# Hybrid DeltaNet and attention block: SBUF start addresses of the matmul operands, byte 0 or byte 32 of a 64-byte line

## The chip, the cores and the metric

The kernel runs on one core of one Trainium2 chip. The metric is device time in microseconds of one execution. Before the change three runs took 1934.67, 1937.08 and 1939.23 us, the median is 1937.08.

## What is computed

One layer of a backbone over 1024 latent tokens with a prefix of 256 context tokens, model width 1024, all in float32. A modulated RMS norm feeds one wide input projection; its columns go to two branches, whose outputs are gated, merged and projected once more.

```python
h  = rms_norm(x)   * (1 + scale)   + shift        # 1024 latent tokens
hc = rms_norm(ctx) * (1 + scale_c) + shift_c      # 256 context tokens
qkv_a, z_a, a_raw, b_raw, q_b, k_b, v_b, z_b, gates = split_cols(h @ w_in)
o_a = gdn_bidirectional(...)     # short conv on q, k, v, then a chunked gated delta rule, both ways, 8 heads
o_b = diff_attend(q, k, v, lam)  # softmax(q1 k1) - lam * softmax(q2 k2), times v, 8 heads, 1280 keys
merged = g_a * (y_a @ w_oa) + g_b * (y_b @ w_ob)
x + gate * (merged @ w_out)
```

## The kernel before

A float32 product is made from three matmuls of float32r operands (the type that TensorE streams faster than float32): each operand is split into a high part and a low part, and high·high, high·low and low·high are summed in one PSUM bank. ScalarE makes the high part with a copy, VectorE or GpSimd the low part with a subtraction. So most matrix tiles come in pairs: `wh` and `wl` (weights), `hs` (two tiles, the normed tokens turned to columns), `ah` and `al` (the softmax weights turned), `vh` and `vl` (values).

Every matmul has two operands in SBUF. The stationary one, 128 columns, is loaded into the array by an instruction of its own (LDWEIGHTS; the profile has it on PEld): this is the *loaded* operand. The other one is *moving*: it is streamed through in 256 or 512 columns (288 for one tile of weights that carries 32 gate columns). Tiles hold float32, so 16 columns are 64 bytes of a partition.

The stages overlap, in this order:

- **Front** (`front`, line 238): loads, RMS norm (`x`), turns through TensorE (`pt`, line 63), modulation with fp32 matmuls of the tile `wa` against `pad` (`mp`), first projection.
- **Convolution** (`conv_flow`, line 496): q, k and v columns of the DeltaNet branch. Here the weights are loaded and `hs` moves, in 512 columns (256 for the context). Two pairs of tiles of `self.wab` take the weights in turn (`conv_weights`, line 488). Between them, for the value columns of the attention (kind `"t"`), `hs` is loaded and the weights move, in 256 columns.
- **q, k, v of the attention** (`part_flow`, line 930, weights by `part_weights`, line 898): `hs` is loaded, weights move, 256 columns.
- **Gates and DeltaNet scan** (`fill_flow`, line 906, and `scan`, line 1292): the gate columns' matmuls, `hs` moving in 512 columns, fill the time between small fp32 matmuls of the scan (`chain`, `out`, `gram`, 128 columns), which TensorE runs in two passes.
- **Attention** (`scores`, line 1536, and on): `s` (loaded `qh` or `ql`, moving `kk`, 512 or 256 columns), turns of the softmax weights (`t`, loaded `S`), `v` (loaded `vh` or `vl`, moving `ah` or `al`, 256 columns). The `ma` matmuls (moving `y`, 512 columns) are put between them.
- **Last products** (`b_main`, line 1909, and `o_main`, line 2097): `mb`, `x` and `z`, all of 512 columns.

The order of the instructions on each engine is worked out while the program is built, by `flow` and `turn_flow` (lines 75 and 100), from costs written into each step; tiles are handed out by pools, some on the left and some on the right side of SBUF (`side="right"`). A pool's tiles lie behind one another, so the length of an early tile sets the start of all that follow on its side. Two such tiles matter here. `mhalf` (line 203) is the one-column constant of the power function, early on the left side. `kq` (in `keys`, line 1093) is an early tile on the right side, and is allocated 8 columns longer than it is used:

```python
self.mhalf = cp.tile([P, 1], F32, name="mhalf")
...
kq, qk = S("kq", [P, LT + L + 8])[:, :LT + L], S("qk", [P, 2, 2, 2, P])
```

Of the kernel before, what the change touches and what calls it, by code (L numbers as in the profile page):

```python
# [8 lines left out]
F32 = mybir.dt.float32  # L9
F32R = mybir.dt.float32r  # L10
# [7 lines left out]
P = 128  # L18
D = 1024
KT = D // P  # L20
L = 1024
LC = 256
LT = L + LC
# [6 lines left out]
W = 256  # L30
# [13 lines left out]
class Block:  # L44
# [150 lines left out]
    def setup(self):  # L195
        nc, a = self.nc, self.a
        cp = self.cp = self.pool("const")
        self.dp = self.pool("spill", space=DRAM)
        ct = cp.tile([P, 3, P], F32, name="ct")
        nc.sync.dma_start(ct, a["consts"].rearrange("(a p) n -> p a n", p=P))  # L200
        self.ident, self.up, self.lo = (ct[:, i, :] for i in range(3))
        self.one = self.lo[:, 0:1]
        self.mhalf = cp.tile([P, 1], F32, name="mhalf")
        nc.gpsimd.memset(self.mhalf, -0.5)
        self.da = self.dp.tile([H, 2 * NT, 4, 32, 32], F32, name="da")
        self.db = self.dp.tile([H, 2 * NT, 4, 32, 32], F32, name="db")
        self.ya = self.dp.tile([2, H, P, L], F32, name="ya")
        self.yb = self.dp.tile([H, P, L], F32, name="yb")
        self.gkq = self.dp.tile([H, P, LT + L], F32, name="gkq")
        self.gkk = self.dp.tile([H, LT, P], F32, name="gkk")  # L210
        self.gv = self.dp.tile([H, LT, P], F32, name="gv")
        self.sza = self.dp.tile([H, P, L], F32, name="sza")
        self.szb = self.dp.tile([H, P, L], F32, name="szb")
        self.qd = self.dp.tile([2, H, P, L], F32, name="qd")
        self.kd = self.dp.tile([2, H, P, LT], F32, name="kd")
        self.vd = self.dp.tile([2, LT, H * P], F32, name="vd")
        self.gt = self.dp.tile([2 * KT, P, L], F32, name="gt")
        self.ma = self.dp.tile([KT, P, L], F32, name="ma")
        self.xq = self.dp.tile([H, P, 2, NT // 2, 2, 2, P], F32, name="xq")
        self.tbd = self.dp.tile([2, P, 1024], F32, name="tbd")  # L220
        self.gcd = self.dp.tile([2, H, LT], F32, name="gcd")
        self.gad = self.dp.tile([1, D], F32, name="gad")
        self.rbd = self.dp.tile([H, L], F32, name="rbd")
        for n in ("gkq", "gkk", "gv", "sza", "szb", "qd", "kd", "vd", "gt", "gcd", "ya", "yb"):
            self.dbg[n] = getattr(self, n).name


    @staticmethod
    def later(t, us):

        return t[0], t[1] + us

    def bank(self, name):

# [3 lines left out]
    def front(self, st, early, kv0):  # L238

        nc, a, cp, V = self.nc, self.a, self.cp, self.nc.vector  # L240
# [67 lines left out]
        def weights():  # L308
            for i, n in ((0, W), (1, W + 32)):
                yield lambda: (f"w{i}", 1) in T  # L310
                hl, ends = [self.wab[1 - i].tile([P, KT, n], F32R, tag=t, name=t) for t in ("wh", "wl")], []
                for s in range(2):
                    k = slice(s * KT // 2, (s + 1) * KT // 2)
                    for o, rw, us in ((0, raws[s], 0.256), (W, grw[:, k], 0.032))[:1 + i]:
                        c = slice(o, o + rw.shape[2])
                        t1 = yield ACT, 0.1 + 3.6 * us, [T[f"w{i}", s], T.get(("mm", 3))], lambda: nc.scalar.copy(hl[0][:, k, c], rw)
                        t2 = yield DV2, 4.7 * us, [t1], lambda: V.tensor_tensor(
                            hl[1][:, k, c], rw, hl[0][:, k, c].bitcast(F32), ALU.subtract)
                        ends += [t1, t2]
                    self.raw_t[s] = t2  # L320
                    if i == 0:
                        T["w", s] = [t1, t2]
                T["hl"] = T.get("hl", hl)
                if i:
                    self.parts_[1] = *hl, ends
# [122 lines left out]
    def conv_start(self, cols, right, late):  # L448

        self.copyq, self.tapq, self.siluq, self.normq, self.evq = [], [], [], ([], []), []  # L450
        self.copied, self.out_t, self.cdone, self.sq_t = {}, {}, set(), [None, None]
        self.row_t, self.sides, self.ringed = None, 0, 0
        self.ctiles = sum(2 for kind, _ in cols if kind in range(3))
        pools, last = self.wab, len(cols) - 1
        for q, b in ((self.copyq, 0), (self.tapq, 1), (self.siluq, 2), (self.normq[0], 2.5), (self.normq[1], 2.5), (self.evq, 0)):
            self.stream(self.forever(q), b)
        for g, b in ((self.gates(), 0.5), (self.lam_setup(), 0.6), (self.qk_tables(), 4), (self.gate_row(), 4)):
            self.stream(self.side(g), b)
        self.stream(self.conv_weights([c for _, c in cols], pools), 3)
        self.stream(self.conv_flow(cols), 9)  # L460
        done = lambda: len(self.cdone) >= self.ctiles and self.sides == 4 and not self.ringed
        self.stream(self.first(done, right, late), 6)
        self.turn_flow(lambda: last in self.parts_ and self.parts_done == last and self.head and not self.evq)
        self.ahead = self.parts_.pop(last)
        self.wab = pools if last % 2 else pools[::-1]
        self.streams = []
# [18 lines left out]
            x = next(g) if callable(x) else g.send((yield x))  # L485
        self.head = g, x

    def conv_weights(self, cols, pools):
        raw = lambda s: (self.wr.tile([P, KT // 2, W], F32, tag="wr", name="wr"), self.raw_t[s])
        for i, c0 in enumerate(cols):  # L490
            if i > 1:
                yield lambda: self.parts_done >= i - 1
                yield from self.weight(raw, *(pools[(i + 1) % 2].tile([P, KT, W], F32R, tag=n, name=n) for n in ("wh", "wl")),
                                       c0, W, [self.part_t.get(i - 2)], self.parts_, i, (DV2, DV2))

    def conv_flow(self, cols):
# [401 lines left out]
    def part_weights(self, parts):  # L898
        raw = lambda s: (self.wr.tile([P, KT // 2, W], F32, tag="wr", name="wr"), self.raw_t[s])
        for i, p in enumerate(parts):  # L900
            if i:
                yield lambda: self.parts_done >= i - 1
                yield from self.weight(raw, *(self.wab[i % 2].tile([P, KT, W], F32R, tag=n, name=n) for n in ("wh", "wl")),
                                       self.part_cols(*p), W, [self.part_t.get(i - 2)], self.parts_, i, (POOL, DV2))

    def fill_flow(self, todo):
# [178 lines left out]
    def gdn_prep(self, h):  # L1085
# [6 lines left out]

        def keys():
            S = lambda nm, shape: self.gh[0].tile(shape, F32, tag=nm, name=nm)
            kq, qk = S("kq", [P, LT + L + 8])[:, :LT + L], S("qk", [P, 2, 2, 2, P])
            kT, qT = kq[:, :LT], kq[:, LT:]
            tk = yield DMA, 3.3, self.kT_t, lambda: nc.sync.dma_start(kq, self.gkq[h])
            tk = tq = self.later(tk, 1.5)
            return kT, qT, qk, tk, tq
# [5 lines left out]
        for d in range(2):  # L1105
            for c in range(NT):
                t = yield ACT, 0.293, [self.later(ld, 2.0)], lambda: nc.scalar.activation(
                    X[:, d, c], X[:, d, c], AF.Abs, bias=self.gcc[:, c, d * H + h:d * H + h + 1], scale=-1.0)
            te[d] = yield ACT, 1.18, [t], lambda: nc.scalar.activation(X[:, d], X[:, d], AF.Exp, scale=-1.0), AF.Exp
        yield lambda: self.gram == h  # L1110
        kT, qT, qk, tk, tq = mine or (yield from keys())

        tX, tQ = [[], []], []
        for c0 in range(0, NT, 2):
# [3 lines left out]
            for j in range(2):  # L1118
                c = c0 + j
                kc = kT[:, c * P:(c + 1) * P]  # L1120
                t = yield PE, 0.2235, [tk, b], lambda: self.mm(pt[:, j * 256:j * 256 + P], kc, kc)
                if c < NL:
                    t = yield PE, 0.2235, [tk, tq, b], lambda: self.mm(pt[:, j * 256 + P:j * 256 + 256], kc, qT[:, c * P:(c + 1) * P])
# [11 lines left out]
            if c0 < NL:  # L1135
                t = yield DMA, 0.91, tQ[-2:], lambda: nc.sync.dma_start(self.xq[h][:, :, c0 // 2, 1], qk[:, c0 // 2 % 2])
# [18 lines left out]
        for j in range(31):  # L1155
            n, w = 31 - j, j + 1
# [470 lines left out]
    def high(self, y, b, k, pt, t, bank):  # L1627

        nb, q = min(4, NT - 4 * k), slice(b * P, b * P + P)
        if b == 0:  # L1630
            yield lambda: self.open_ and self.vdone[k] >= y["i"]
            for a in ("ah", "al"):
                y[a, k] = self.a1.tile([P, nb, W], F32R, tag=f"{a}{k}", name=a)
            y["old", k], y["in", k] = self.vfree[k], []
        pv = pt[:, :nb * P].rearrange("p (j f) -> p j f", f=P)
        e = yield ACT, 0.48 if nb == 4 else 0.27, [t, y["old", k]], lambda: self.nc.scalar.copy(y["ah", k][:, :, q], pv)  # L1636
        self.lows.append((2 * y["i"] + 1, self.low(y, k, pv, q, e, bank)))
# [573 lines left out]
```

## Time and profile before

| what | value |
|---|---|
| median of three runs | 1937.08 us |
| the profiled execution | 1935.46 us |
| its span, first to last instruction | 1933.3 us |
| TensorE busy, matmuls | 1896.7 us, 13807 instructions |
| TensorE busy, loads | 1675.3 us, 13807 instructions |
| VectorE, ScalarE, GpSimd busy | 1453.0, 1062.6, 678.8 us |
| DMA | 336.39 MB, 174 GB/s on average |

How to read the profile: it is of one execution. PE is TensorE's matmuls, PEld its loads, DVE VectorE, ACT ScalarE, POOL GpSimd, SP the queue that issues DMAs. A group's line names the source line, engine, operation, output and inputs, their shape and the count, then busy time, mean duration of one in ns, and idle time of the engine just before. The lines 56 and 63 are the helpers that issue every matmul and every turn, so matmuls are told apart by their tiles. A matmul's recorded duration runs from its start to its modelled end and overlaps that of the next one. A row of the timeline or of the chain has the start, the time it covers, and the number of instructions merged in it. A row of a window has the window, its length, then for PE, PEld, DVE, ACT and POOL the busy time with the count, the granted clock, the DMA share and its rate.

### The profile page before, as it was taken

The page shows a single profiled execution, that of the slowest core. Times are in us where ns is not written, and L with a number is a line of the kernel's source. Part 1 is how long each engine was busy: PE and PEld are TensorE (multiplying, and loading weights), DVE is VectorE, ACT ScalarE, POOL GpSimd, SP SyncE. Part 2 cuts the span into 40 slices and gives each one's busy share as a digit, 9 for nine tenths or more (in the row PEclk, how much of TensorE's full clock was granted, in tenths as well). Part 3 has the DMA queues.
Part 4 walks back from the last instruction along what each step waited for, and adds up shares of the span by engine and source line. Part 5 has one row for each costly group of instructions (what it writes and reads, how often), then busy time and mean ns, then how long its engine had stood idle before and what let it go on. Part 6 is the DMA issues. An engine that isn't in the chain of part 4 may idle for free.

```text
span 1933.3 us, 37454 instructions
## 1 busy us (share of the span) xinstructions
PE 1896.7 (98%) x13807; PEld 1675.3 (87%) x13807; DVE 1453.0 (75%) x3613; ACT 1062.6 (55%) x2189; POOL 678.8 (35%) x610
## 2 busy tenths in 40 slices
PE   6999999999999999999999999999999999999999
PEld 4878888899999998888888888888997888888887
DVE  4687998957887887867865865338996979995677
ACT  4543444426233563677576645439885868884222
POOL 3200000005441342343333332336766667672203
PEclk9999999999999999999999999999999999999999
DMA  9144535575545567667785565666336474226542
GB/s 335 58 137 96 138 95 138 123 190 179 165 142 183 183 191 228 216 204 232 213 292 175 195 199 150 212 231 224 132 124 210 158 238 151 93 88 213 186 157 87
DMA packets 383038, 336.39 MB, mean 174 GB/s; under 512 B 142609, under 2 KB 323443, under 8 KB 381831
## 3 DMA queue, kind: packets, MB, share of 16 engines
q1 hardware_dynamic: 382855, 333.99, 55.0%
q8 instruction: 109, 1.79, 0.4%
q14 instruction: 74, 0.61, 0.1%
HBM read 222.14 MB, written 111.79 MB: 173 GB/s over the span
## 4 chain that ended last, share of the span: by engine, by line
PE 84%; DVE 6%; DMA 4%; ACT 3%; issue 2%; SPq 1%; POOL 1%; DVEq 0%; ACTq 0%; POOLq 0%
PE mm L56 43%; PE s L56 7%; PE v L56 5%; PE chain L56 5%; PE mb L56 5%; PE ma L56 4%; PE x L56 3%; PE t L63 3%; PE out L56 3%; PE gram L56 1%; DVE S L1567 1%; DVE ac L595 1%; PE pz L56 1%; PE tr L63 1%; SPq L265 1%
## 5 line engine op out<-in xcount | busy, mean ns | idle before, releaser
L56 PE MATMUL mm<-hs,wh 128*128 128x512 f32 (+1 forms) x2048 | 648.7, 390 | 1.5 <-DVE hs L408 1.4
L56 PEld LDWEIGHTS mm<-hs,wh 128*128 128x128 f32 x2048 | 371.3, 189 | 58.7 <-DVE hs L408 2.0
L56 PE MATMUL mm<-hs,wl 128*128 128x512 f32 (+1 forms) x1024 | 397.8, 388 | 1.0 <-POOL wl L886 1.0
L56 PE MATMUL mm<-wh,hs 128*128 128x256 f32 (+1 forms) x1792 | 332.7, 286 | 0.2 <-ACT sq L978 0.2
L56 PEld LDWEIGHTS mm<-wh,hs 128*128 128x128 f32 x1792 | 281.0, 191 | 0.7 <-ACT sq L978 0.4
L1567 DVE TENSOR_SCALAR_CACHE_REDUCE S<-s,rsq 128x512 f32<-128x512 f32 (+1 forms) x384 | 239.8, 655 | 26.9 <-DMA vl<-vd 12.0
L56 PE MATMUL mm<-wl,hs 128*128 128x256 f32 (+1 forms) x896 | 256.0, 286 | 0.0
L1604 POOL TENSOR_TENSOR S<-S 128x1280 f32<-128x1280 f32 x64 | 188.9, 2955 | 92.2 <-ACT S L1597 90.9
L56 PEld LDWEIGHTS mm<-hs,wl 128*128 128x128 f32 x1024 | 194.0, 189 | 29.8 <-POOL wl L886 1.4
L1580 ACT ACTIVATE S<-S,mn 128x1280 f32<-128x1280 f32 x128 | 175.2, 1372 | 51.3 <-DVE mn L1579 50.9
L56 PEld LDWEIGHTS mm<-wl,hs 128*128 128x128 f32 x896 | 171.4, 191 | 0.1
L595 DVE SCALAR_TENSOR_TENSOR ac<-xc,convT,ac 128x1284 f32<-128x1284 f32 (+1 forms) x96 | 138.8, 1448 | 11.2 <-ACT ac L593 10.6
L56 PE MATMUL s<-kk,qh 128*128 128x512 f32 (+1 forms) x384 | 142.7, 372 | 1.9 <-DVE S L1567 1.7
L56 PE MATMUL s<-kk,ql 128*128 128x512 f32 (+1 forms) x384 | 132.9, 358 | 0.0
L1641 DVE TENSOR_TENSOR al<-t,ah 128x512 fp32r<-128x512 f32 (+1 forms) x192 | 107.0, 595 | 7.6 <-ACT ah L1636 6.3
L580 POOL MEMSET xc<- 128x2 f32 (+1 forms) x64 | 3.6, 100 | 298.5 <-ACT sq L629 113.1
L1160 DVE TENSOR_TENSOR ts<-ts,tmp 80x31 f32<-80x31 f32 (+15 forms) x248 | 94.1, 380 | 6.0
L1323 ACT ACTIVATE vd<-chain,edk 128x128 f32<-128x128 f32 x144 | 52.2, 370 | 77.8 <-PE chain L56 71.9
L56 PE MATMUL ma<-y,wh 128*128 128x512 f32 x256 | 93.0, 410 | 1.7 <-DVE g L1814 1.7
L1158 DVE TENSOR_TENSOR tmp<-ab,ts 80x31 f32<-80x31 f32 (+15 forms) x248 | 89.2, 360 | 6.6 <-DMA ab<-da 1.3
L1636 ACT CAST ah<-t 128x512 fp32r<-128x512 f32 (+1 forms) x192 | 87.9, 521 | 9.0 <-PE t L63 8.3
L56 PE MATMUL v<-al,vh 128*128 128x256 f32 x320 | 90.9, 284 | 0.7 <-DVE al L1641 0.6
(296 smaller groups left out, 4315.7 us busy)
## 6 DMA issues: line engine op xcount, KB each, us to landing
wr<-in_w_in_dram SPq DMA_DIRECT2D x48, 512.0 KB, 5.7
hx<-in_w_in_dram SPq DMA_DIRECT2D x64, 256.0 KB, 4.3
x<-xq SPq DMA_DIRECT2D x64, 256.0 KB, 5.1
X<-gcd SPq DMA_DIRECT2D x8, 1280.0 KB, 7.1
kd<-col SPq DMA_DIRECT2D x40, 256.0 KB, 2.2
xq<-X SPq DMA_DIRECT2D x16, 640.0 KB, 8.9
kk<-kd SPq DMA_DIRECT2D x16, 640.0 KB, 6.4
kq<-gkq SPq DMA_DIRECT2D x8, 1152.0 KB
```

The costliest lines, as they stand in the source:

```text
L56: self.nc.tensor.matmul(out, lhsT, rhs, start=start, stop=stop)
L63: self.nc.tensor.transpose(out, src, self.ident[:src.shape[0], :src.shape[0]])
L265: return DMA, us, list(deps), lambda: nc.sync.dma_start(dst, src)
L595: t = yield DV2, 1.21e-3 * wd, [t], lambda: nc.vector.scalar_tensor_tensor(ac[:, :wd], xc[:, j:j + wd], self.convw(j, x["ct"]), ac[:, :wd] ...
L1158: t = yield DV2, n * w / 960.0 + 0.08, [t if j else self.later(t, 2.5), t1], lambda: V.tensor_tensor(tv, ab[:, j + 1:, j:j + 1].to_broadca ...
L1160: t = yield DV2, n * w / 960.0 + 0.08, [t, t1], lambda: V.tensor_tensor(ts[:, j + 1:, :w], ts[:, j + 1:, :w], tv, ALU.subtract)
L1323: td = yield ACT, 0.251, [t], lambda: nc.scalar.activation(vd, pc[:, 1], AF.Copy, scale=self.edk[:, c, g:g + 1])
L1567: e = yield DVE, 0.675 if m == 512 else 0.408, [e, self.sfree[c].get(n - 4 + c)], lambda: self.nc.vector.tensor_scalar(x["S"][c][:, o:o + ...
L1580: x["x"].append((yield ACT, 1.36, [e], lambda: nc.scalar.activation(S, S, AF.Exp, bias=x["mn"][:, c:c + 1], scale=-1.0, accum_out=w["l0"][ ...
L1604: e = yield POOL, 2.9, [e], lambda: self.nc.gpsimd.tensor_tensor(S0, S0, S1, ALU.add)
L1636: e = yield ACT, 0.48 if nb == 4 else 0.27, [t, y["old", k]], lambda: self.nc.scalar.copy(y["ah", k][:, :, q], pv)
L1641: t = yield DVE, 0.603 if k < 2 else 0.322, [e, y["old", k]], lambda: self.nc.vector.tensor_tensor(y["al", k][:, :, q], pv, y["ah", k][:, ...
```

## The change

Only start addresses change; all instructions, their order on each engine and their waits are those of before.

- `mhalf` is allocated 9 columns long, of which the first is used: every later tile on the left side starts 32 bytes further on.
- The 8 spare columns of `kq` are dropped: tiles behind it on the right side start 32 bytes away from where they did.
- A helper `at` allocates a tile with 16 spare columns (64 bytes) and hands out a view that starts `off` columns into it. With `off` 8 the view starts 32 bytes after the tile, which takes it back to byte 0 of a 64-byte line; with `off` 0 it starts where the tile does, at byte 32.
- `at` with 8 is used for weights that move in 256 or 288 columns (in the front for the second tile, in `conv_weights` for the kinds that are not q, k or v of the DeltaNet branch, in `part_weights` for all) and for `ah` and `al`. Weights that are loaded keep `off` 0.

In the built program before, both operands of every float32r matmul start at byte 0 of a 64-byte line. After it, all their loaded operands start at byte 32; moving operands of 512 columns at byte 32; moving `wh`, `wl`, `ah`, `al` at byte 0; `hs` and `kk` where they move in 256 columns, 640 matmuls, at byte 32. The float32 operands move along: scan tiles go from byte 0 to byte 32, the turns' moving identity stays at byte 0.

```diff
-        self.mhalf = cp.tile([P, 1], F32, name="mhalf")
+        self.mhalf = cp.tile([P, 9], F32, name="mhalf")[:, 0:1]
...
+    @staticmethod
+    def at(pool, k, n, tag, off, name):
+
+        return pool.tile([P, k * n + 16], F32R, tag=tag, name=name)[:, off:off + k * n].rearrange("p (k n) -> p k n", k=k)
...
-                hl, ends = [self.wab[1 - i].tile([P, KT, n], F32R, tag=t, name=t) for t in ("wh", "wl")], []
+                hl, ends = [self.at(self.wab[1 - i], KT, n, t, 8 * i, t) for t in ("wh", "wl")], []
...
-        self.stream(self.conv_weights([c for _, c in cols], pools), 3)
+        self.stream(self.conv_weights([c for _, c in cols], pools, [i for i, (k, _) in enumerate(cols) if k not in range(3)]), 3)
...
-                yield from self.weight(raw, *(pools[(i + 1) % 2].tile([P, KT, W], F32R, tag=n, name=n) for n in ("wh", "wl")),
+                yield from self.weight(raw, *(self.at(pools[(i + 1) % 2], KT, W, n, 8 if i in moving else 0, n) for n in ("wh", "wl")),
...
-                yield from self.weight(raw, *(self.wab[i % 2].tile([P, KT, W], F32R, tag=n, name=n) for n in ("wh", "wl")),
+                yield from self.weight(raw, *(self.at(self.wab[i % 2], KT, W, n, 8, n) for n in ("wh", "wl")),
...
-            kq, qk = S("kq", [P, LT + L + 8])[:, :LT + L], S("qk", [P, 2, 2, 2, P])
+            kq, qk = S("kq", [P, LT + L]), S("qk", [P, 2, 2, 2, P])
...
-                y[a, k] = self.a1.tile([P, nb, W], F32R, tag=f"{a}{k}", name=a)
+                y[a, k] = self.at(self.a1, nb, W, f"{a}{k}", 8, a)
```

More of the change, by code (lines that the diff above doesn't have):

```diff
@@ L486, in first, with conv_weights @@
         self.head = g, x
-    def conv_weights(self, cols, pools):
+    def conv_weights(self, cols, pools, moving):
         raw = lambda s: (self.wr.tile([P, KT // 2, W], F32, tag="wr", name="wr"), self.raw_t[s])
```

## The prediction

> **What bounds the kernel now.** I read the page first: the busy shares, the slices, the chain that ended last.
>
> ```profile
> span 1933.3 us, 37454 instructions
> PE 1896.7 (98%) x13807; PEld 1675.3 (87%) x13807; DVE 1453.0 (75%) x3613; ACT 1062.6 (55%) x2189; POOL 678.8 (35%) x610
> PE   6999999999999999999999999999999999999999
> PEclk9999999999999999999999999999999999999999
> PE 84%; DVE 6%; DMA 4%; ACT 3%; issue 2%; SPq 1%; POOL 1%; DVEq 0%; ACTq 0%; POOLq 0%
> PE mm L56 43%; PE s L56 7%; PE v L56 5%; PE chain L56 5%; PE mb L56 5%; PE ma L56 4%; PE x L56 3%; PE t L63 3%; PE out L56 3%; PE gram L56 1%; DVE S L1567 1%; DVE ac L595 1%; PE pz L56 1%; PE tr L63 1%; SPq L265 1%
> ```
>
> TensorE is busy from the second slice to the end at full clock and holds 84% of the chain. So time comes off mainly by starting matmuls closer together. A matmul's recorded duration overlaps its neighbour's, so its price is the distance from start to start. The chain in order of time gives that distance where nothing interrupts: 256-column matmuls of a projection, then 512-column ones of the last stage.
>
> ```profile
> 399.98 34.53 PE mm L56 x288
> ```
> ```profile
> 1766.26 87.04 PE mb L56 x384
> 1875.06 10.88 PE z L56 x48
> ```
>
> 34.53 us / 288 = 119.9 ns for 256 columns; 87.04 / 384 = 226.7 ns for 512, and 10.88 / 48 = 226.7 again. The additional 256 columns cost 226.7 − 120.0 = 106.7 ns, 0.417 ns each. So 512 columns stream in 213.3 ns and 256 in 106.7, and each matmul pays the same surplus of 13.3 ns whatever its length. It is this surplus that an address could change; the columns themselves can't go.
>
> How many pay it stands in the groups by line with shapes kept apart.
>
> ```profile
> L56 PE MATMUL mm<-hs,wh 128*128 128x512 f32 x1792 | 602.2, 405 | 1.5 <-DVE hs L408 1.4
> L56 PE MATMUL mm<-hs,wl 128*128 128x512 f32 x896 | 361.5, 403 | 1.0 <-POOL wl L886 1.0
> L56 PE MATMUL mm<-wh,hs 128*128 128x256 f32 x1632 | 300.5, 285 | 0.2 <-ACT sq L978 0.2
> L56 PE MATMUL mm<-wl,hs 128*128 128x256 f32 x816 | 232.3, 285 | 0.0
> L56 PE MATMUL s<-kk,qh 128*128 128x512 f32 x256 | 106.2, 415 | 1.6 <-DVE S L1567 1.4
> L56 PE MATMUL ma<-y,wh 128*128 128x512 f32 x256 | 93.0, 410 | 1.7 <-DVE g L1814 1.7
> L56 PE MATMUL v<-al,vh 128*128 128x256 f32 x320 | 90.9, 284 | 0.7 <-DVE al L1641 0.6
> L56 PE MATMUL ma<-y,wl 128*128 128x512 f32 x128 | 52.3, 409 | 0.0
> L56 PE MATMUL mb<-yh,wl 128*128 128x512 f32 x128 | 49.8, 389 | 0.0
> L56 PE MATMUL mm<-hs,wh 128*128 128x256 f32 x256 | 47.0, 284 | 0.0
> L56 PE MATMUL x<-bh,al 128*128 128x512 f32 x96 | 37.4, 389 | 0.0
> L56 PE MATMUL s<-kk,qh 128*128 128x256 f32 x128 | 36.6, 286 | 0.3 <-DVE S L1567 0.2
> L56 PE MATMUL mm<-hs,wl 128*128 128x256 f32 x128 | 36.3, 283 | 0.0
> L56 PE MATMUL mm<-wh,hs 128*128 128x288 f32 x160 | 32.3, 296 | 0.0
> L56 PE MATMUL mm<-wl,hs 128*128 128x288 f32 x80 | 23.6, 295 | 0.0
> L56 PE MATMUL z<-bl,ah 128*128 128x512 f32 x16 | 6.2, 389 | 0.0
> ```
>
> Of 512 columns: 1792 + 896, two s groups of 256, 256 + 128 for ma, three mb groups of 128, three x groups of 96, three z groups of 16: 4304. Of 256: 1632 + 816, three v groups of 320, 256 + 128, two s groups of 128: 4048, and 160 + 80 of 288. In all 8592. Their surplus is 8592 × 13.3 = 114 us, 6% of the span.
>
> How much of a saving arrives: the chain holds mm 43 + s 7 + v 5 + mb 5 + ma 4 + x 3 = 67% of 1933.3 us, 1295 us, and 10.9 us of z. The pace makes 4304 × 226.7 + 4048 × 120.0 + 240 × 133.3 = 1493 us of these matmuls. So 1306 / 1493 = 0.875 of their time is on the chain, and I count 0.875 of every saving or loss per matmul.
>
> **The change, part by part.** No instruction is added, removed or moved; addresses alone change. Widening mhalf moves every later tile of the left side by 32 bytes, dropping the pad of kq those of the right side. In the program before, both operands of all 8592 matmuls start at byte 0 of a 64-byte line. After it every loaded operand starts at byte 32, the moving ones of 512 columns too, and the moving weights and softmax tiles of 256 columns (and the 288) stay at byte 0. The 640 matmuls of 256 columns with hs or kk moving go to 32.
>
> *Other engines and DMA: nothing.* Before has tiles at both places in one group: the 512-column transposes of L609 work from and to byte 0 and byte 32, and the scalings of L1597 likewise.
>
> ```profile
> L609 DVE STREAM_TRANSPOSE xc<-ac x64: 390/702/712, 97.0 to 412.3; 128x512 f32<-128x512 f32 x48, 128x256 f32<-128x256 f32 x16
> ```
> ```profile
> L1597 ACT ACTIVATE S<-S,rl x48: 1349/1368/1418, 1314.6 to 1740.3; 128x1280 f32<-128x1280 f32 x48
> ```
>
> Median and longest lie 1 to 4% apart (the 390 is the 256-column form), so VectorE and ScalarE do not see the half line. For a DMA, a row of 2 KB would touch one 64-byte line more in 33: on the chain's 4% of DMA that is 0.04 × 1933 / 32 = 2.4 us at most, and none if nothing waits. I take 0.
>
> *Fp32 transposes and passes: nothing.* In the front, pt loads x from byte 32; in the attention, t loads S from byte 0; the moving identity is at byte 0 in both. And mp streams 256 fp32 columns from byte 32 (at 35.74) or byte 0 (at 43.15).
>
> ```profile
> 51.47 0.82 PE L63 MATMUL pt<-ct,x 128*128 128x128 f32 x6
> ```
> ```profile
> 1402.63 0.93 PE L63 MATMUL t<-ct,S 128*128 128x128 f32 x7
> ```
> ```profile
> 35.74 1.07 PE L56 MATMUL mp<-wa,pad 128*32 128x256 f32 x16
> ```
> ```profile
> 43.15 1.07 PE L56 MATMUL mp<-wa,pad 128*32 128x256 f32 x16
> ```
>
> With the last one's 0.27 us taken off, (0.82 − 0.27) / 5 = 0.110 and (0.93 − 0.27) / 6 = 0.110 us: a load of 128 columns costs 0.11 us from either byte. The mp blocks take 1.07 us from either. So byte 32 costs a load nothing when loads set the pace, and slow streaming nothing.
>
> *The 8592 matmuls: the one unknown.* All of them have both operands at byte 0, so no row prices their change. From below: 110 ns between loads is the nearest floor for 256 columns, 10 ns less than 120, and 8592 × 10 × 0.875 = 75 us gained. From above, the slowest uninterrupted rows, in the attention:
>
> ```profile
> 1401.37 0.40 PE L56 MATMUL s<-kk,qh 128*128 128x512 f32 x1
> ...
> 1402.07 0.39 PE L56 MATMUL s<-kk,ql 128*128 128x512 f32 x1
> 1402.29 0.28 PE L56 MATMUL s<-kk,qh 128*128 128x256 f32 x1
> 1402.40 0.28 PE L56 MATMUL s<-kk,ql 128*128 128x256 f32 x1
> ```
>
> Three matmuls of 512 in 0.70 us are 233 ns, 6.7 above 226.7, while a 256 just behind took 110: the surplus is no constant of the engine, it depends on how load and stream meet, and 6.7 ns more on 8592 is 50 us lost.
>
> Between the ends I choose by size. A load passes 128 columns in 0.110 us, 0.86 ns a column; the 16 fp32 columns of a 64-byte line take 13.8 ns, close to the 13.3 ns that every matmul pays. I read the surplus as the load's first line, which must be there before the stream can be handed over. At byte 32 that line holds 8 columns, and the surplus halves to 6.7 ns: 120 becomes 113.3, 226.7 becomes 220. That is an argument from a coincidence of sizes, hence the modest chance. Saved: 8592 × 6.7 = 57.3 us, × 0.875 = 50.1.
>
> Then nothing else is late: in the two fullest stages the other engines have room for 3%.
>
> ```profile
> 60.00:380.00 320.00, 316.82 (x1672) 271.00 (x1671) 269.96 (x411) 136.39 (x172) 7.30 (x69) 1.00 0.45 117
> 1330.00:1740.00 410.00, 405.48 (x2646) 358.39 (x2647) 354.37 (x1202) 327.62 (x553) 277.20 (x139) 1.00 0.47 156
> ```
>
> The third count is VectorE's: 84% and 86%. The profiled execution took 1935.5 us, 2.2 outside its span, and lies 1.6 under the median of 1937.1. 1935.5 − 50.1 = 1885.4, and 1.6 for the median: **1887 us**.
>
> **The rivals.**
>
> *No effect (0.17): 1937 us.* The pt, t and mp rows speak for it: neither load nor stream noticed the half line. Against it, those matmuls do not pay the surplus at all. [...]
>
> *Slower (0.21): 1966 us.* If the stream pays by the line it touches, 512 columns from byte 32 touch 33 lines for 32. One line is 16 columns × 0.417 = 6.7 ns, the very step by which the s rows are late. The 4304 pay it and the 640 that go to byte 32 with 256 columns; those kept at byte 0 pay nothing: 4944 × 6.7 × 0.875 = 29 us. It decides the sign once it exceeds what the loads gain. Against it: mp from byte 32 was no slower, though it streams at half rate.
>
> *Only those with the moving operand kept at byte 0 gain (0.17): 1916 us.* They alone get their two operands at different halves of a line; the others stay side by side, as before. 4288 − 640 = 3648, × 6.7 × 0.875 = 21 us.
>
> *The whole surplus goes but for the loads' floor (0.11): 1862 us*, the 75 us above. [...]
>
> **How the numbers follow.** The forecast has 0.34. A measurement of this kernel can tell about 0.2%, 4 us, from no change. Faster: 0.34 + 0.17 + 0.11 = 0.62; same 0.17; slower 0.21. Low: 1855, just under the whole-surplus case, leaves out 0.04. High: 1966, the slower case's own price, leaves out half of its 0.21. Range 1855 to 1966; the likeliest case's own range is 1878 to 1897.
>
> **What would show it.** Right: the mb run of 384 lasts 84.5 us for 87.04, the mm run of 288 lasts 32.6 us for 34.53, pt, t and mp stand, the span loses 50 us in proportion to the count of these matmuls. If mb stands and mm shortens, it is the rival in which only unlike halves gain; if mb grows to 89.6, the slower one. Wrong altogether: both runs shorten and the span does not, so another engine was next; or DMA waits grow in the chain.

## The result, and the profile after

| | before | after |
|---|---|---|
| median of 15 runs | 1935.31 us (1934.03 to 1939.23) | 1939.21 us (1936.88 to 1943.83) |
| profiled execution | 1935.46 us | 1940.55 us |
| its span | 1933.3 us | 1938.4 us |

The ratio after to before is 1.0017, 95% interval 1.0009 to 1.0025. So nothing came of the 50 us: the change makes the kernel slower by 3 to 4 us, which lies inside the 0.2% that the prediction called no change.

The page of after, the lines that answer to those of before:

```profile
span 1938.4 us, 37453 instructions
PE 1898.9 (98%) x13807; PEld 1669.7 (86%) x13807; DVE 1454.6 (75%) x3613; ACT 1062.7 (55%) x2189; POOL 678.6 (35%) x610
PE   6999999999999999999999999999999999999999
PEclk9999999999999999999999999999999999999999
PE 58%; DVE 5%; ACT 1%; issue 1%; DMA 1%; POOL 0%; SPq 0%; DVEq 0%; POOLq 0%; ACTq 0%
```

TensorE is as busy as before (1898.9 us for 1896.7) and at full clock (granted 1.00 up to 1880 us, 0.99 behind it). The shares of the chain sum to 66% because here it could be followed back only to 660 us; they do not compare with the 84%, its rows behind 660 us do. Two runs of matmuls of the chain before, one of 512 columns in the convolution stage (42 matmuls) and one of 256 in the q, k, v stage (95):

```profile
209.92 9.65 PE mm L56 x42
...
714.99 11.39 PE mm L56 x95
```

The same places after the change, the second run and the last stage from the chain:

```profile
717.37 11.26 PE mm L56 x95
...
1771.29 87.05 PE mb L56 x384
...
1880.11 10.88 PE z L56 x48
```

and the run of 42 from the timeline of TensorE, where it lies between two small products: the row behind the first one, and the row of the second.

```profile
211.02 0.71 PE L56 MATMUL mm<-hs,wh 128*128 128x512 f32 x2
...
220.85 0.31 PE L56 MATMUL pq<-ks,fold 128*128 128x40 f32 x2
```

The 256-column run gained, 119.9 to 118.5 ns a matmul. The 512-column run of the last stage stands at 226.7. And the 512-column run of the convolution lost: 220.85 − 211.02 = 9.83 us for what took 9.65, 234.0 ns a matmul for 229.8. The groups show the same two directions (mean ns of one: 405, 403, 285 and 285 before):

```profile
L56 PE MATMUL mm<-hs,wh 128*128 128x512 f32 x1792 | 605.0, 406 | 1.5 <-DVE hs L413 1.4
L56 PE MATMUL mm<-hs,wl 128*128 128x512 f32 x896 | 364.9, 407 | 1.0 <-POOL wl L891 1.0
L56 PE MATMUL mm<-wh,hs 128*128 128x256 f32 x1632 | 296.8, 282 | 0.3 <-ACT sq L983 0.3
L56 PE MATMUL mm<-wl,hs 128*128 128x256 f32 x816 | 231.4, 284 | 0.0
```

Counted from start to start over all uninterrupted neighbours of the two traces, mm<-hs,wh of 512 columns went from 228.3 to 230.5 ns and mm<-hs,wl from 228.6 to 234.4; with 256 columns mm<-wh,hs from 119.8 to 117.6, mm<-wl,hs from 119.8 to 119.4; mb, x and z stayed. Each distance is counted here to the matmul that starts first; counted to the one that starts next, the loss splits into 4.3 and 1.6 ns, with the same sum. 1792 × 2.2 + 896 × 5.8 = 9.1 us lost, 1632 × 2.2 + 816 × 0.4 = 3.9 us gained, and some 2 us more in the smaller groups of 256.

All other work stands, as the prediction had it: in the timeline mp, then t with (1.03 − 0.27) / 7 = 0.109 us a turn, and VectorE's transposes by line.

```profile
35.98 1.07 PE L56 MATMUL mp<-wa,pad 128*32 128x256 f32 x16
...
1407.47 1.03 PE L63 MATMUL t<-ct,S 128*128 128x128 f32 x8
```
```profile
L614 DVE STREAM_TRANSPOSE xc<-ac x64: 390/703/716, 96.9 to 415.7; 128x512 f32<-128x512 f32 x48, 128x256 f32<-128x256 f32 x16
```

Where on the way the time is lost shows when the start of the same matmul (the n-th on TensorE, whose order is the same in all these kernels) is compared. The table has us later than before (minus: earlier) at eight places, for after and for the experiments below:

| place in before, us | after | E2 | E3 | E4 | E7 | E8 | E10 |
|---|---|---|---|---|---|---|---|
| 60 | +0.3 | +0.3 | 0.0 | +0.4 | +1.0 | −0.1 | −0.4 |
| 380, end of convolution | +3.4 | −0.9 | +2.9 | +2.4 | 0.0 | −1.0 | −1.6 |
| 560 | +2.4 | −0.9 | +3.3 | +0.9 | −3.7 | −2.1 | −1.5 |
| 740, end of q, k, v | +2.2 | −0.2 | +3.6 | +0.6 | −3.8 | −2.4 | +1.7 |
| 1190, end of gates and scan | +5.4 | +1.3 | +3.6 | +2.0 | −4.4 | −1.0 | +2.2 |
| 1330 | +5.0 | +1.0 | +3.3 | +1.5 | −3.3 | −1.2 | +2.1 |
| 1740, end of attention | +4.9 | +1.1 | +3.4 | +1.5 | −4.2 | −1.5 | +2.0 |
| 1929, end | +5.1 | +1.4 | +3.7 | +1.7 | −4.3 | −1.4 | +2.2 |

After loses 3.1 us in the convolution, where 512 columns move, regains 1.2 where 256 do, and loses 3.2 in the gates stage: there the 512-column matmuls take 1.8 us more, and TensorE's waits grew from 3.0 to 4.1 us. Such waits differ by 1 to 2 us between single executions (E3 has 1.7), so a step of that size in one column proves nothing.

### The profile page after: what moved, and what is told of

Same layout as the page of the kernel before. It is cut to its first block, busy times and chain, and to the rows that moved or that the text cites. A ratio compares the mean times of both kernels' runs of the same rounds, so it can differ in the third digit from the quotient of the medians.

```text
span 1938.4 us, 37453 instructions
## 1 busy us (share of the span) xinstructions
PE 1898.9 (98%) x13807; PEld 1669.7 (86%) x13807; DVE 1454.6 (75%) x3613; ACT 1062.7 (55%) x2189; POOL 678.6 (35%) x610
## 3 DMA queue, kind: packets, MB, share of 16 engines
q1 hardware_dynamic: 382855, 333.99, 55.4%
## 4 chain that ended last, share of the span: by engine, by line
PE 58%; DVE 5%; ACT 1%; issue 1%; DMA 1%; POOL 0%; SPq 0%; DVEq 0%; POOLq 0%; ACTq 0%
PE mm L56 20%; PE s L56 7%; PE v L56 5%; PE chain L56 5%; PE mb L56 4%; PE ma L56 4%; PE x L56 3%; PE t L63 3%; PE out L56 3%; DVE S L1572 1%; PE gram L56 1%; PE pz L56 1%; DVE al L1646 1%; PE z L56 1%; ACT S L1585 0%
## 5 line engine op out<-in xcount | busy, mean ns | idle before, releaser
L56 PE MATMUL mm<-wh,hs 128*128 128x256 f32 (+1 forms) x1792 | 328.8, 283 | 0.3 <-ACT sq L983 0.3
```

What stands on the lines that cost most here:

```text
L56: self.nc.tensor.matmul(out, lhsT, rhs, start=start, stop=stop)
```

## The experiments

**What was to be told apart.** The helper `at` did two things: it chose byte 0 or 32, and its 16 spare columns made every tile 64 bytes longer. In the built program the four weight tiles of the projection (wh, wl, wh, wl), all at the same place before, stand 0, 64, 128 and 192 bytes further on than `hs` within 256 bytes. Theory 1: byte 32 harms the 512-column runs. Theory 2: the displacement of the tiles against each other does.

**E2, all at byte 32** without spare columns (against before):

```diff
-        self.mhalf = cp.tile([P, 1], F32, name="mhalf")
+        self.mhalf = cp.tile([P, 9], F32, name="mhalf")[:, 0:1]
...
-            kq, qk = S("kq", [P, LT + L + 8])[:, :LT + L], S("qk", [P, 2, 2, 2, P])
+            kq, qk = S("kq", [P, LT + L]), S("qk", [P, 2, 2, 2, P])
```

> All operands of the large products at byte 32 of a 64-byte line, without the spare columns behind each tile: high and low tile of a pair stand at the same byte of 128, and the 256-column weights stream from byte 32 too. Theory 1 (byte 32 under both operands is what slows the 512-column runs): their paces stay as after the change (230 to 234 ns in the conv and gates stages), the 256-column ones go back to 120.0 if unlike halves made their gain, so 1941 to 1944 us. Theory 2 (the 64 bytes between high and low tile): the 512-column runs go back to 226.7 to 229 ns as before, so 1933 to 1936 us. If the gain of the 256-column ones came from the loaded side alone, 5 us less in either case.

Measured: 1937.40 us against 1936.55, ratio 1.0003 (0.9994 to 1.0012). The two runs of the chain:

```profile
209.06 9.65 PE mm L56 x42
...
714.78 11.38 PE mm L56 x95
```

Both as before, and so are the paces of all groups (228.3, 228.5, 119.8, 119.8). Byte 32 as such does nothing, neither good nor bad. Theory 1 falls, and with it the reason behind the forecast.

**E3, the spare columns alone** (the changed kernel's helper, every offset 0, nothing else changed from before):

```diff
+        return pool.tile([P, k * n + 16], F32R, tag=tag, name=name)[:, :k * n].rearrange("p (k n) -> p k n", k=k)
```

> The spare 16 columns behind each tile alone, no operand moved to byte 32: high tiles at byte 0 as before, low tiles at byte 64 of 128. Theory 2: the 512-column matmuls that load the low tile go from 227.7 to 229 ns up to 232 to 234, the 256-column ones stay at 119.8, so some 1941 to 1945 us. Theory 1: no operand stands at byte 32, so nothing changes: 1934 to 1937 us.

Measured: 1941.34 against 1936.55, ratio 1.0020 (1.0011 to 1.0028).

```profile
210.69 9.83 PE mm L56 x42
...
718.64 11.39 PE mm L56 x95
```

The run of 42 takes 9.83 us, to the last digit that of after. Group by group the 512-column paces are those of after within 0.2 ns (230.6 and 234.3 for 230.5 and 234.4). So the whole loss of the change comes from its spare columns. One expectation failed: the 256-column matmuls did not all stay, mm<-wh,hs went to 118.9, so these too follow the displacement.

**E4, the changed kernel with high and low tile of a pair at the same byte of 128:**

```diff
-        return pool.tile([P, k * n + 16], ...
+        return pool.tile([P, k * n + (32 if tag == "wh" else 16)], ...
```

> The changed kernel with 32 spare columns behind the high tiles of the weights in place of 16, so that high and low tile of a pair stand at the same byte of 128 (loaded 32 and 32 or 96 and 96, moving 0 and 0 or 64 and 64); all else as after the change. Theory 2: the 512-column matmuls return to 227 to 229 ns and the 256-column ones keep their 1 to 2 ns, so 1928 to 1932 us, faster than before by 0.2 to 0.4%. Theory 1: the 512-column ones stay at 230 to 234, so 1937 to 1941 us.

Measured: 1938.67 against 1936.55, ratio 1.0014 (1.0005 to 1.0024).

```profile
210.50 9.79 PE mm L56 x42
...
715.83 11.13 PE mm L56 x95
```

This is a miss: the 512-column run is still at 233.1 ns. Agreement within 128 bytes is not what counts. In the built program the tiles of a pair, wh and wl, now stand 0 and 128 bytes from hs within 256, and those of the other pair 192 and 64; E5 was made to find the length that matters.

**E1 and E5, the matmuls alone.** No other engine works beside them; the loop is that of the kernel, one load for each matmul:

```python
for i, (x, y) in enumerate(((0, 0), (0, 1), (1, 0))):
    nc.tensor.matmul(bank[:, :n], S[x][:, k * P:(k + 1) * P], M[y][:, c:c + n],
                     start=k == i == 0, stop=k == K - 1 and i == 2)
```

> This kernel leaves out the whole computation of the reference and issues float32r matmuls alone: 32 uninterrupted runs of 96, each matmul with a new load of 128 columns (high tile with high and low moving tile, then low with high). 16 blocks, each once behind four transposes (PSUM tiles ta to tp) and once behind one fp32 matmul (fa to fp). Blocks a to h have 512 moving columns, i to p 256; bytes within 128 of the loaded high, loaded low, moving high, moving low tile: a 0 0 0 0; b 32 32 32 32; c 32 96 32 32; d 0 64 0 0; e 32 32 0 0; f 0 0 32 32; g 64 64 0 0; h 0 0 0 64; i 0 0 0 0; j 32 32 64 0; k 32 32 0 0; l 32 32 64 64; m 32 32 32 32; n 0 0 32 32; o 0 0 32 96; p 0 0 64 0. Theory 1 (byte 32 under both operands keeps a 512-column run from settling at 226.7 ns): a, d, g, h at 226.7, b and c at 230 to 234. Theory 2 (what costs is that the two loaded tiles lie 64 bytes apart within 128): c and d at 230 to 234, a and b at 226.7. Theory 3 (the 256-column ones gain where load and stream stand in unlike halves of a 64-byte line): i, m, p at 120.0, k, l, n, o near 117.6; if the loaded side alone gains, m goes as k and n stays at 120. The forecast's reason (a load pays 6.7 ns less from byte 32) gives b and e 220, k 113.3. No difference between blocks: the paces come from what runs beside the matmuls in the full kernel.

From its chain, the blocks a, c and i:

```profile
39.69 22.19 PE fa L52 x96
...
129.97 22.38 PE fc L52 x96
...
390.70 11.31 PE fi L52 x96
```

Neither theory's numbers came out: c, with the low tile 64 bytes off, is slower than a (233.1 for 231.1), but a is not at 226.7 nor i at 120.0. Only afterwards did I see why: there the low tiles lie 128 bytes from the high ones within 256 in every block, before a block's own bytes are added. E5 puts them all at one multiple of 256. E1 also shows that addresses are not quite all: block k, the same operands twice, took 118.9 ns a matmul behind four transposes and 118.3 behind one fp32 matmul.

```profile
425.91 11.42 PE tk L52 x96
...
437.55 11.37 PE fk L52 x96
```

> Leaves out the whole computation again: 32 runs of 96 float32r matmuls, each behind one fp32 matmul, all operands in one tile that starts at a multiple of 512 bytes. PSUM tiles aa to ap: 512 columns; ba to bp: 256. Bytes within 512 of loaded high, loaded low, moving high, moving low: aa 0 0 0 0; ab all 32; ac 0 0 32 32; ad 32 32 0 0; ae 0 64 0 0; af 32 96 32 32; ag 0 128 0 0; ah 0 256 0 0; ai 0 0 64 64; aj 0 0 128 128; ak 0 0 256 256; al 0 0 0 128; am 0 0 0 64; an 0 0 16 16; ao 0 0 224 224; ap 32 160 32 32; ba all 0; bb all 32; bc 32 32 0 0; bd 0 0 32 32; be 64 64 0 0; bf 128 128 0 0; bg 256 256 0 0; bh 96 96 0 0; bi 16 16 0 0; bj 192 192 0 0; bk 224 224 0 0; bl 0 0 224 224; bm 32 32 64 0; bn 0 64 0 0; bo 0 0 0 64; bp 0 128 0 0. Theory now (where load and stream stand to each other within 256 or 512 bytes sets the pace, not the byte of the 64-byte line): aa, ab, ak at 226.7 and ba, bb at 120.0 as in the kernel before, and the ones with a tile 64 or 128 off at 230 to 234 and 115 to 119; those with the moving pair off by 32 tell whether the 256-column runs can gain while the 512-column ones keep 226.7. Rival (only the 128-byte place of the low tile counts): aj, ag, al at 226.7, ae, af, am at 233. Rival (other engines' work in the full kernel makes the difference): aa not at 226.7, as none of the first matmul kernel's blocks was.

```profile
39.52 21.79 PE ab L50 x96
...
61.53 22.39 PE ac L50 x96
...
106.75 22.17 PE ae L50 x96
...
173.97 21.79 PE ah L50 x96
...
195.98 21.99 PE ai L50 x96
...
375.39 11.52 PE ba L50 x96
...
398.86 11.36 PE bc L50 x96
...
421.87 10.90 PE be L50 x96
...
444.61 11.52 PE bg L50 x96
```

Divided by 96, and with the first few left out: all at one byte, or 256 apart, 226.7 ns for 512 columns (ab, ah) and 120.0 for 256 (ba, bg), the numbers of the kernel before to the tenth. Every other distance is slower for 512 columns: 233.3 (ac, the stream 32 bytes further on), 231.1 (ae, only the low loaded tile 64 off), 228.9 (ai). For 256 columns every other distance is at most as slow: 118.3 with the load 32 bytes further on than the stream (bc), and 113.3 with 64 (be). Nothing but addresses differs between the blocks, and moving all of them together by 32 bytes, or one side by 256, changes nothing: what moves the pace is the distance of load and stream within 256 bytes.

**E6, more distances:**

> Leaves out the whole computation, as the run before it: runs of 96 float32r matmuls from one tile at a multiple of 256 bytes. ww: 512 columns, all at 0. ca to cl: 512 columns, both loaded tiles at 4, 8, 16, 48, 56, 64, 80, 96, 128, 160, 208, 240, the moving ones at 0; da to dl: 256 columns, loaded at 4, 8, 48, 56, 72, 80, 112, 144, 160, 176, 208, 240. The last four of each (cm to cp, dm to dp): loaded high, low, moving high, low at 64 64 0 64; 64 0 0 0; 0 64 0 64; 64 128 0 0. Theory (load and stream of one matmul collide by their distance within 256 bytes; loads 64 bytes ahead of the stream came out at 113.3 for 256 columns): paces change smoothly around 64 (56 and 72 near 114, 48 and 80 near 115 to 117), and the mixed cases lie between; for 512 columns 64 gives 220 if the load's stay in one phase is what counts, 230 to 234 if the second half of the stream, which the load does not meet, decides. Rival (only whole 32-byte or 64-byte steps count): 4 and 8 read as 0 does, 48 and 56 as 32.

```profile
84.49 22.39 PE cc L51 x96
...
152.37 22.40 PE cf L51 x96
...
287.96 21.93 PE cl L51 x96
...
411.65 11.11 PE db L51 x96
...
434.57 11.31 PE dd L51 x96
...
446.10 11.36 PE de L51 x96
```

The loads 16 or 64 bytes further on give 233.3 for 512 columns (cc, cf), at 64 the opposite of what they do for 256; no distance tried beat 226.7 there (next is 228.3, cl, 240). For 256 columns 64 is a single point: 56 and 72 give 117.8 and 118.3 (dd, de), while 8 gives 115.6 (db). The smooth curve that I expected is not there, and the rival's steps of 32 bytes aren't either.

The distance is not the whole account. Where all operands stand at multiples of 32 bytes, pairs of blocks with the same distance agree within 0.2 ns (bc and bl 118.3, bd and bk 116.7, aj and ci 232.5 and 232.3). But E5's block an, whose stream is 16 bytes further on than the load, and E6's cl, whose load is at 240 and stream at 0, have the same distance within 256 and run at 231.7 and 228.3 ns. What else counts there is open.

```profile
307.90 22.24 PE an L50 x96
```

**E7, the distance that E5 found best.** Moving tiles of 256 columns stand 64 bytes behind the loaded ones, all else keeps its byte within 256 (the spare columns of a pair sum to 256 bytes). Against before, with uses as in the change; `rr`, the last tile of that pool, is 16 columns longer, so that the tiles behind keep their places:

```diff
+    def at(self, pool, k, n, tag, moving=False):
+
+        if pool is self.wa:
+            pad, off = (48, 48 * moving) if tag == "wh" else (16, 16 * (not moving))
+        else:
+            pad, off = (48, 48 * moving) if n == W else (0, 0)
+        return pool.tile([P, k * n + pad], F32R, tag=tag, name=tag)[:, off:off + k * n].rearrange("p (k n) -> p k n", k=k)
...
         self.a1 = self.spool(st, "a1")
+        self.a1.tile([P, 48], F32, name="pad")
```

> The kernel before, with one kind of move: tiles that stream 256 columns (weights of q, k, v; softmax tiles) stand 64 bytes behind the loaded ones within 256 bytes (byte 192 for 0), by spare columns that sum to 256 bytes, so that every other operand keeps its byte, and all 512-column matmuls keep load and stream at the same byte of 256. Theory (distance of load and stream within 256 bytes): the 2448 matmuls with a moving weight tile go from 119.8 to near 113.4 ns, the 512-column ones stay at 226.7 to 229, the 960 of v fall by up to 6 ns where they run undisturbed. 2448 x 6.4 ns x 0.875 = 13.7 us, and up to 4 us more from v: 1917 to 1924 us. Rival (the matmuls alone are no guide to the full kernel, where other engines use the same memory): under 3 us, 1933 to 1938. Rival (the time that the matmuls give back is taken by the evictions behind them): paces fall to 113.4 but the time by less than half, 1929 to 1934.

Measured: 1929.12 us (1926.48 to 1934.50) against 1935.62, ratio 0.9970 (0.9960 to 0.9979). Faster than both kernels, by 6.5 us where 12 to 19 were expected; it stands at the edge of the last rival's range, in which the paces fall and the time by less than half. Its chain:

```profile
209.97 9.65 PE mm L56 x42
...
562.92 27.10 PE mm L56 x239
...
711.64 10.78 PE mm L56 x95
```

The 512-column run is back at 9.65 us. The run of 239 has 113.4 ns a matmul, that of 95 has 113.5 for 119.9. Over the stage, the 256-column matmuls at full clock take 114.4 ns for 119.8: 2448 × 5.4 = 13 us. The table shows 3.8 us of it at 740, and the trace has the terms of the difference. In two stretches 27 matmuls ran at 213 ns, 2.7 us in all, with the granted clock down:

```profile
600.00:620.00 20.00, 20.00 (x231) 19.61 (x231) 18.13 (x47) 9.43 (x27) 1.45 (x4) 1.00 0.45 149
620.00:640.00 20.00, 18.03 (x146) 17.83 (x145) 12.33 (x30) 12.26 (x31) 5.86 (x3) 0.91 0.82 279
```

(the second window has 0.91 where the first has 1.00). And TensorE's idle time between 380 and 740 us went from 2.1 to 5.7 us. The longest wait of that stage before, and now:

```profile
PE tr L63 <- DVE fin L1000: 1.0, 1, 1.0
```
```profile
PE tr L63 <- DVE fin L1009: 2.2, 2, 2.0
```

Of these 3.6 us more, 2.5 stand before the turns (tr), which wait for the rotated q and k tiles (fin) that VectorE and GpSimd make: matmuls that end sooner wait longer for them. Counted from each start to the next without the waits, the 2448 took 8.5 us less than before in this execution (the half clock included; that the 1.8 us still missing, 13 − 2.7 − 8.5, are matmuls behind an interruption that gain less is the author's estimate), the turns and gram matmuls of the stage 1.1 us more: −8.5 + 1.1 + 3.6 = −3.8. Between 1330 and 1740 only 0.9 us is gained: the v matmuls, uninterrupted at 116.5 ns for 118.8, gave 1.8 us there, of which the s matmuls took 0.6 and longer waits 0.3.

**E8, a lead of 32 bytes**, 56 and 8 in place of 48 and 16: what the change gives its 256-column weights, without the displacement of the rest.

> What the change set out to do for its 256-column matmuls, without its side effect: tiles that stream 256 columns stand 32 bytes behind the loaded ones (224 for 0 within 256 bytes), the spare columns sum to 256 bytes, and all 512-column matmuls keep load and stream at the same byte of 256. Theory (distance within 256 bytes sets the pace, as the matmuls alone showed: 118.3 ns for loads 32 ahead): the 2448 of the moving weights fall from 119.8 to near 118.3, the 512-column ones stay at 226.7 to 229 ns: 2448 x 1.5 x 0.875 = 3 us less than before, 1931 to 1934 us. Rival (byte 32 as such harms the 512-column runs or the eviction): 1937 to 1940, as after the change.

Measured: 1934.52 against 1936.70, ratio 0.9988 (0.9979 to 0.9997).

```profile
208.92 9.65 PE mm L56 x42
...
712.74 11.24 PE mm L56 x95
```

9.65 us, and 118.3 ns for the 256-column run, E5's value for this distance. The expected 3 us came as 2.2.

**E9, the lead of 64 for the weights alone** (E7 without the two edits of the attention's pool):

> The 64-byte lead for the streamed weights alone, the softmax tiles at their old byte. If the attention stage is not bound by its v matmuls (in the run with both it ended no earlier against the stages before), this gives what both gave: 1927 to 1931 us. If v had its share, 2 to 3 us more than with both, 1931 to 1934. If the clock drops again where the 256-column matmuls run at 113.3 ns (stretches at 213 ns in the run with both), the drop belongs to the faster pace; if it does not, it was chance.

Measured: 1932.48 us (7 runs) against 1936.70, ratio 0.9977 (0.9964 to 0.9990). It lies where a share of v was expected, but it does not tell E7 and E9 apart with certainty, since the intervals overlap (0.9960 to 0.9979 for E7). Its trace gains nothing between 1330 and 1740, where that of E7 gains 0.9 us. It also has 23 matmuls at half clock, near 640 us (0.90 granted from 620 to 640, 0.93 from 640 to 660).

**E10, spare columns in phase.** The tiles of E7's weights, but views at the same byte of 256 for both uses:

```diff
+            pad, off = (48, 0) if tag == "wh" else (16, 16)
```

> The spare columns alone, every operand back at the byte of 256 that it had before: tiles of the weights are as wide as with the 64-byte lead, but loaded and streaming views start at the same byte. Theory (what the spare columns of the change did, they did by moving the low tile and the tiles behind it against the others): 512-column runs at 226.7 to 229, 256-column ones at 119.8, 1934 to 1937 us. Rival (a wider tile by itself costs, by its strides or what it waits for): 1938 to 1941, as the run with the spare columns alone.

Measured: 1936.13 against 1936.70, ratio 0.9994 (0.9985 to 1.0002).

```profile
208.36 9.65 PE mm L56 x42
...
716.69 11.38 PE mm L56 x95
```

As before. Longer tiles cost nothing where they keep the phase; this closes E3's question. Here too 16 matmuls ran at half clock (600 to 603 us, 0.92 granted from 600 to 620), at the old pace.

**The drops of the clock.** By the word of E9's expectation the drop belongs to the faster pace if it comes again there, and it came; E10 shows that the faster pace is not needed for it. The granted clock that is on record for every execution, as a mean over it, tells how often the clock was lowered: one drop of 3.4 us to half clock makes it 0.999. It is below 1.000 in 15 of the 18 executions of E7 and E9, in 9 of 66 of the kernel before that ran beside the experiments, and in 14 of 70 of all other kernels (1 of 11 each in E8 and E10). So the drop happens at the old pace too, but is far more frequent where the 256-column matmuls run at 113 to 115 ns. The two executions of E7 without one took 1926.48 and 1926.89 us, some 9 us less than before, against 6.5 for the median of all eleven. In the three traces that have drops (E7, E9, E10), each begins within 0.9 us of the end of a wait of TensorE of 1.5 to 2.8 us, before p or tr. Waits of 1.6 to 1.9 us at the same places passed without one in after, E3, E4 and E8, so a long wait alone does not decide, and what does stays open.

## Why the prediction was wrong

- **What bounds the kernel** was right: TensorE at full clock (98% busy after too), and start-to-start distance as the price. E7 (ratio 0.9970) and E8 (0.9988) took time off by nothing else, E3 (1.0020) put it on.
- **The surplus of 13.3 ns that each matmul pays, "the same whatever its length"**: the numbers were right, the reading as a constant wrong. Over the 106.7 and 213.3 ns that it worked out for the columns, 13.3 is what two operands at the same byte of 256 pay. E5 and E6 have 6.7 to 13.3 at 256 columns (113.3 to 120.0), and 13.3 to 21 at 512. The s rows at 233 ns, from which the prediction saw that the surplus varies, are not explained by this: in the built program before, half of the ql matmuls stand 64 bytes from kk within 256 and half at 0, and both take 232 to 233 ns.
- **Other engines, DMA, fp32 passes, transposes: nothing.** Right: mp stays at 1.07 us, a turn takes 0.109 us for 0.110, the median of L614 is 703 ns for 702; VectorE, ScalarE and GpSimd are busy 1454.6, 1062.7 and 678.6 us for 1453.0, 1062.6 and 678.8, and the packets of the main DMA queue took 55.4% for 55.0% of the span of 16 engines.
- **The failed step** is the choice among the bounds: "I read the surplus as the load's first line, which must be there before the stream can be handed over. At byte 32 that line holds 8 columns, and the surplus halves to 6.7 ns". E2 moved every load to byte 32 and all paces stayed (228.3, 228.5, 119.8 and 119.8 ns); in E5 the surplus is 13.3 with all operands at byte 32 (ab, 226.7 ns) as at 0. The coincidence of sizes was one. The 6.7 does exist, in block be, but it comes from the load's distance to the stream, 64 bytes, and only for 256 columns.
- **What was overlooked**: the part on the change said that loaded operands go to byte 32 and named the bytes within 64. The 16 spare columns, which set each later tile's place, were read in the diff and not priced. They made all of the loss (E3, 1.0020 where the change has 1.0017).
- **No effect (0.17)** came nearest in the number, 1937 for 1939.2, and its reason, that neither load nor stream notices the half line, holds for byte 32 itself: E2's ratio is 1.0003. It has nothing on the distance of load and stream, where a shift of 16 bytes took 512 columns from 226.7 to 233.3 in E6 (block cc). So the near zero in this case is a sum of two effects, about 9 us of pace lost and 6 gained, of which the path kept +3 to +5 us.
- **Slower (0.21)**: 512-column matmuls did lose, by 2.2 and 5.8 ns where it had 6.7, but not since the stream touches one line more: mb, x and z stream from byte 32 as well and stand at 226.7.
- **Only those with the moving operand kept at byte 0 gain (0.17)** is half right: they gained, but 0.4 to 2.2 ns for 6.7, and not they alone. The context's 256-column matmuls, with hs moving at byte 32 like its load, went from 119.6 to 117.3 ns (mm<-hs,wh), and went there in E3 too, with both at byte 0: that is the spare columns' work. What unlike halves bring by themselves is E8's 1.5 ns.
- **The whole surplus goes (0.11)**: no run came near. The smallest surplus measured, over the same 106.7 ns and with a load for each matmul, is 6.7 ns (block be, 113.3 for 256 columns).
- **What would show it**: mb at 87.05 for 87.04 and the 256-column runs shorter is the sign that it named for the rival of unlike halves. That sign was too coarse: it held no 512-column run of the convolution, where the loss is.
- **0.875 of a saving arrives**: for the loss it came near, (9.1 − 6) × 0.875 = 2.7 us where the interval of the ratio has 1.7 to 4.8. For E7's gain it did not: 13 us of pace gave 6.5, since TensorE's waits in that stage grew by 3.6 us in the traced execution and the clock dropped more often.

## What to carry to other kernels

Where a matmul loads and streams at once, look at the distance of the two tiles, not at the byte of either, and at every tile that a longer one pushes along: here a pad of 64 bytes behind each tile (E3, 1.0020) cost more than the distance of 32 bytes that it served could bring (E8, 0.9988), and longer tiles are harmless by themselves (E10, 0.9994). Pads that sum to the period (256 bytes in these runs: 226.7 and 120.0 ns at distance 256 as at 0) keep all the rest in place. A blind price taken from a coincidence of two sizes deserves a micro-measurement, or a smaller chance; 96 matmuls in a row, with nothing but addresses changed, settled it.

## What the runs showed of the hardware that was not expected

- The start-to-start distance of float32r matmuls, each with its own load, depends on the distance of the loaded and the moving tile within 256 bytes: 226.7 to 234.4 ns at 512 columns (least at distance 0 and 256), 113.3 to 120.0 at 256 columns (least where the load is 64 bytes further on; 120.0 at 0 and 256, and also at 112, 144, 160 and 240).
- It repeats: the kernels' runs of 42, 95 and 239 matmuls gave 9.65, 11.38 or 11.39 and 28.66 or 28.67 us wherever the distances were those of before. It is not the whole account: the same distance gave 231.7 and 228.3 ns in blocks an and cl.
- One distance can serve one length and harm the other: loads 64 bytes further on took 256 columns from 120.0 to 113.3 and 512 columns from 226.7 to 233.3. Why is not shown here.
- Between 595 and 643 us some executions ran 16 to 27 matmuls at half pace (213 ns for 256 columns), with the granted clock at 0.90 to 0.93 over 20 us. Some lowering of the mean clock is on record in 15 of 18 executions with a lead of 64 bytes and in 9 of 66 of the kernel before: here the faster pace went with a clock that was lowered more often.
